# Issue order in a hybrid attention and Fourier encoder: one block of projection steps, the statistics of the next chunk, roundings, late weights and first loads are moved

## The chip, the cores and the metric

The kernel runs on one core of one Trainium2 chip. The metric is the device time of one execution in microseconds (us), the median of several runs. A difference of about 0.3% (4.9 us here) is what a measurement of this kernel can tell from no change.

TensorE is called PE below, its weight loads PEld; VectorE is DVE, ScalarE is ACT, GpSimd is POOL, and SyncE, which only issues transfers in this kernel, is SP. A "q" behind such a name is the engine's sequencer, which issues transfers and waits.

## The reference

```python
def attention_layer(x, g, w_in, w_out, sink, rel_bias):
    h = rmsnorm(x, g)
    z = h @ w_in                               # q, k, v and gate
...
    o = banded_gqa_with_sink(q, k, v, rel_bias, sink)
    return x + (o * jax.nn.silu(gate)) @ w_out

def fourier_layer(x, g, w_gate, w_out):
    h = rmsnorm(x, g)
    f = jnp.fft.fftn(hg, axes=(1, 3), norm="ortho").real   # over positions, and over each group of 256 channels
...
    return x + (f * jax.nn.silu(h @ w_gate)) @ w_out
```

Both layers run once, attention first, and a last rmsnorm follows. This is done for a prompt of 2048 positions and, apart from it, for a sample of 512 positions; the model width is 1024. Attention has 16 query heads of 64 channels, four to each key and value head, looks 128 positions back and ahead, adds a bias per distance and head, and counts one learned sink per head in the sum under the softmax. All values are float32.

## The kernel before, in words

Every float32 product is made as three products of rounded parts: a value is split into a high part (a cast by ACT) and a low part (a subtraction by DVE or POOL), and `matmul3` (lines 92 to 95) multiplies high by high, high by low and low by high. So most tiles come in two parts, and "rounding" below means the cast and the subtraction that follows it.

**Attention.** Positions are cut into five chunks of 512: the sample first (chunk 0), then four of the prompt. For a chunk, `make_h` (187) loads x transposed, one block of 128 channels (k) after the other, and splits it into h. `kv_proj` (287) makes keys and values. The 16 heads then go in eight pairs p; a pair is called a query here. `qg_proj` (369) gives each pair 16 steps on PE, eight for its query and eight for its gate, each step three matmuls over one k; after the eighth step of each half the result is taken out of PSUM (`evac_q`, `evac_g`). `attention` (410) has the parts of one pair's attention over 128-position blocks b: `scores`, `biased` (DVE adds the bias to the scores and finds the extreme value), `exps` (ACT), `divide`, `transp` (PE transposes), `parts` (ACT and DVE round the transposed weights), `av` (PE), `out_evac` (ACT copies half of the result, the tile `t`, DVE adds, POOL multiplies by the gate) and the `split` that `out_evac` returns (ACT rounds the gated result into `uT`, POOL or DVE makes its low part).

The loop over n (800 to 856) writes the order out by hand: 17 periods a chunk, each with two blocks of scores of the new half of a pair and the transposes and products of the half before. Projection steps are spread between them as filler: `ahead_n` steps run before the first period (16 in chunk 0, 12 in the others), the rest is shared out over 27 half periods by `quota`. At the end of each period four numbered extras run (`extra`, 784). Among them are the statistics of the next chunk (`stats`, 151): `one(i)` squares and sums tile i-1 of x on ACT (line 162) and loads tile i (166); when all are summed, `inv_rms` (86) makes the reciprocal roots, the first step on DVE (88), the second on POOL (89). In chunk 0 they start in period 6, in the later chunks in period 9; the fifth chunk has no next one. For chunk 0 itself they run at once, inside `kv_proj`.

**What sets the order.** Each engine runs its instructions in one fixed order. A planner makes that order from the order in the program, by costs that it assumes. `after(a, b)` (128) puts a behind b in the planner's eyes only; `seq(engine, ins)` (133) chains the instruction behind the last chained one of that engine. Scores, biased, exps, divide, parts, projection evacuations, the copy of `t` and the split's cast are all chained in this way. Squares, reciprocal roots, weight casts (114), x loads and weight loads are not: the planner puts them where it believes they fit. `keep_in_program_order` puts an instruction behind everything written before it on its engine.

**The start.** `half` (234) loads the first key weights in two halves, one on SP's and one on ACT's queue, ahead of the x tiles; each half is rounded by ACT (238) and DVE (239). `bias_rows` (247) loads three small tensors for the bias.

**Fourier phase and the turn.** `gates` (998) makes the gates with one level of Strassen's scheme. At the last call, `hooks` (1427 on) put other work between its products: the loads of the output weights (`f_load`, tiles `wo`), and the first Fourier harmonics over positions (`position`, 1195; `halves_of`, 1183, rounds its input `gl` into `gs`, lines 1190 and 1191). Output weights 0 to 7 come as stored parts; the rest is loaded as float32 (`w32f`, line 1412) and rounded by `f_split` (1414; ACT on 1418, DVE on 1419). After the gates come the harmonics 0 and 2 of the sample (`early`) and `finish` (1246), the output projection of two tiles.

Of the kernel before, what the change touches and what calls it, by code (L numbers as in the profile page):

```python
# [43 lines left out]
def encoder(  # L44
# [40 lines left out]

    def inv_rms(ss, n, name):
        inv = main.tile([P, 8], F32, tag="inv", bufs=2, name=name)
        DVE.tensor_scalar(inv[:, :n], ss[:, :n], 1.0 / D, EPS, ALU.mult, ALU.add)
        POOL.tensor_tensor(inv[:, :n], inv[:, :n], mhalf[:, :n], ALU.pow)
        return inv  # L90
# [37 lines left out]
    def after(ins, anchor):  # L128

        if anchor is not None:  # L130
            tc.add_manual_dep(ins.ins, anchor.ins.name, ISSUE, reason="issue order")
# [10 lines left out]
    def attention_phase():  # L142

        with ExitStack() as es:
# [6 lines left out]
            def stats(c):  # L151

                tok, lo_t, hi_t = CHUNKS[c]
                nt = min(640, hi_t - tok) // P
                ss = main.tile([P, 8], F32, tag="ss", bufs=2, name=f"ss{c}")

                xs = []

                def one(i):

                    if i:
                        sq = ACT.activation(xs[i - 1], xs[i - 1], AF.Square, accum_out=ss[:, i - 1 : i])
                        after(sq, last_exp[0])
                    if i < nt:
                        xs.append(xtile([P, D], F32, f"xs{c}_{i}"))
                        after(SP.dma_start(xs[i], x[tok + i * P : tok + (i + 1) * P, :]), last_exp[0])

                return [lambda i=i: one(i) for i in range(nt + 1)] + [lambda: inv_rms(ss, nt, f"inv{c}")]

# [16 lines left out]

            def make_h(c, invb, between={}):

# [3 lines left out]
                for k in range(KD):  # L192
# [4 lines left out]
                    else:  # L197
                        xk = xtile([P, D], F32, f"xk{c}_{k}")[:, :640]
                    SP.dma_start(xk[:, :n], xT[k * P : (k + 1) * P, tok : tok + n])
                    if invb is not None:  # L200
# [32 lines left out]

            def half(i):
                cs = slice(i * 512, i * 512 + 512)
                (SP, ACT)[i].dma_start(wk32[:, cs], w_in[8, :, cs])
                return lambda: (
                    tc.keep_in_program_order(ACT.copy(wk[:, 0, cs], wk32[:, cs])),
                    DVE.tensor_tensor(wk[:, 1, cs], wk32[:, cs], f32(wk[:, 0, cs]), ALU.subtract),
                )  # L240

            halves = [half(i) for i in range(2)]
            halves[0]()
            early = [(wk[:, 0], wk[:, 1])]
            hs, halo = make_h(0, None, {0: halves[1], 3: lambda: early.append(load_w(0, 9, "k0_1", DVE))})

            def bias_rows():

                rowd = dram.tile([NH, 512], F32, name="rowd")
                rb = ap.tile([33, NH], F32, tag="tmp", bufs=2, name="rb")  # L250
                DVE.memset(rb[32:33], 1.0)
                SP.dma_start(rb[:32], rel_bias)
                oh = ap.tile([33, 512], F32, tag="s", bufs=2, name="oh")
                SP.dma_start(oh, onehot)
                bp = bank("bp")
                PE.matmul(bp[:NH], rb, oh, start=True, stop=True)
                brow = ap.tile([NH, 512], F32, tag="tmp", bufs=2, name="brow")
                DVE.tensor_copy(brow, bp[:NH])

                POOL.dma_start(rowd, brow)  # L260
                sk = ap.tile([P, NH], F32, tag="sk", name="sk")
                SP.dma_start(sk, bass.AP(sink.tensor, sink.offset, [[0, P], [1, NH]]))
                DVE.tensor_scalar(sk, sk, -1.0, None, ALU.mult)
                return rowd, sk
# [480 lines left out]
            for c in range(len(CHUNKS)):  # L745
# [22 lines left out]

                ahead_n = 16 if c == 0 else 12
                chain.pop(PE, None)  # L770
# [29 lines left out]
                for n in range(17):  # L800
# [24 lines left out]
                    if new:  # L825
                        for j in range(2):
                            new[0].exps(new[1], j)
                        if n < 15:
                            for j in range(2):
                                new[0].biased(new[1] + 1, j)  # L830
                        new[0].divide(new[1], 0)
                        for j in range(2):
                            new[0].exps(new[1] + 1, j)
                        new[0].divide(new[1], 1)
                        for j in range(2):
                            new[0].divide(new[1] + 1, j)
                    for i in range(quota[2 * n] if n < 15 else 18 - n):
                        (work or op).pop(0)()
                    if split:
                        split()  # L840
                        split = None
                    if old:
# [18 lines left out]
    def fourier_phase(tail):  # L861
        with ExitStack() as es:
# [559 lines left out]
            def turn_first(i):  # L1422
# [9 lines left out]
                4: [lambda: f_load(4)],  # L1432
                5: [lambda: turn_first(0), lambda: f_load(5), lambda: f_split(4)],
                6: [lambda: turn_first(1), lambda: f_split(5)],
            })
            new = [t for p in early for t in position(*p)]
            for k in (6, 7):
# [223 lines left out]
```

## Time and profile before

| | |
|---|---|
| median of three runs | 1619.75 us (1616.98, 1619.75, 1622.47) |
| the profiled execution | 1622.4 us |
| its span, first to last instruction | 1620.6 us |
| mean granted TensorE clock | 0.995 of full speed |

The profile is of one execution. A row of a timeline gives the start in us from the span's start, the length in us, the engine, the line of the kernel, the operation, the tile written and the tiles read, the shapes and the count; in brackets stands how long the engine was idle before it and what ended that. In a shape such as 128x512 the first number is partitions.

### The profile page before, as it was taken

How to read it: one execution, taken by the hardware profiler on the slowest of the kernel's cores; microseconds unless marked ns; L12 is line 12 of the kernel's file. 1: busy time of each engine (PE TensorE's matmuls, PEld its weight loads, DVE VectorE, ACT ScalarE, POOL GpSimd, SP SyncE). 2: the span in 40 equal slices, each digit the busy share in tenths (PEclk: the TensorE clock that was granted, in tenths of full speed). 3: DMA queues.
4: the chain of work that ended last, by engine and by line, in shares of the span. 5: the costliest groups of instructions: out<-in, count | busy, mean ns of one | idle time of the engine just before them, and what ended most of it. 6: DMA issues, size and time to landing. Idle time of an engine off the chain costs nothing.

```text
span 1620.6 us, 27520 instructions
## 1 busy us (share of the span) xinstructions
PE 1598.9 (99%) x9835; PEld 1334.6 (82%) x9835; DVE 1116.6 (69%) x2799; ACT 870.2 (54%) x2043; POOL 431.1 (27%) x605
## 2 busy tenths in 40 slices
PE   9999999999999999999999999999999999999998
PEld 7777888888888888978788888888888887888886
DVE  6788665777547776367754577668576767988696
ACT  6687644676237674157752476546545554343252
POOL 2456551421403414024222242211112111100010
PEclk9999999999999999999999999999999999999999
DMA  7487696656765567655659566666456469455952
GB/s 300 157 314 272 227 351 218 227 215 211 287 220 197 214 237 259 225 205 214 242 166 326 203 219 228 236 217 248 170 208 241 172 220 407 153 195 195 348 201 91
DMA packets 100644, 374.16 MB, mean 231 GB/s; under 512 B 12139, under 2 KB 22379, under 8 KB 83100
## 3 DMA queue, kind: packets, MB, share of 16 engines
q1 hardware_dynamic: 81708, 297.91, 51.8%
q0 software_dynamic: 16464, 70.30, 11.1%
q10 hardware_dynamic: 2336, 4.20, 0.7%
q8 instruction: 78, 1.28, 0.3%
q14 instruction: 58, 0.48, 0.1%
HBM read 281.10 MB, written 91.26 MB: 230 GB/s over the span
## 4 chain that ended last, share of the span: by engine, by line
PE 87%; DMA 5%; DVE 4%; ACT 2%; issue 1%; POOL 1%; SPq 0%; POOLq 0%; DVEq 0%; ACTq 0%
PE qp L95 13%; PE gp L95 12%; PE op L95 8%; PE spt L95 8%; PE W L95 6%; PE spt L441 6%; PE av L525 6%; PE fo L95 5%; PE z L95 4%; PE vp L95 4%; PE Z L95 3%; PE pt L499 3%; PE Wo L95 2%; PE X L95 2%; PE trb L940 1%; DMA xs<-in_x_dram 1%
## 5 line engine op out<-in xcount | busy, mean ns | idle before, releaser
L95 PE MATMUL qp<-h,wq 128*128 128x512 f32 x960 | 239.9, 399 | 0.2 <-DVE pts L508 0.2
L95 PE MATMUL gp<-h,wg 128*128 128x512 f32 x960 | 237.7, 396 | 0.0
L460 DVE CUSTOM_DVE_ANT_0 S<-spt,b 128x385 f32<-128x385 f32 (+1 forms) x320 | 156.9, 527 | 115.6 <-PE spt L441 115.2
L507 ACT CAST pts<-pt 128x384 fp32r<-128x384 f32 (+1 forms) x320 | 123.8, 472 | 185.6 <-PE pt L499 185.4
L95 PEld LDWEIGHTS qp<-h,wq 128*128 128x128 f32 x960 | 176.6, 190 | 42.6 <-issue 5.2
L95 PEld LDWEIGHTS gp<-h,wg 128*128 128x128 f32 x960 | 175.2, 188 | 43.5 <-issue 9.7
L468 ACT ACTIVATE S<-S 128x385 f32<-128x385 f32 (+1 forms) x320 | 190.1, 605 | 35.6 <-DVE S L460 35.1
L508 DVE TENSOR_TENSOR pts<-pt,pts 128x384 fp32r<-128x384 f32 (+1 forms) x320 | 147.3, 522 | 25.7 <-ACT pts L507 24.7
L549 POOL TENSOR_TENSOR uT<-o,uT 128x256 fp32r<-128x256 f32 x75 | 55.5, 740 | 358.9 <-ACT uT L548 358.9
L95 PE MATMUL op<-wo,uT 128*128 128x512 f32 x600 | 140.4, 391 | 0.0
L95 PE MATMUL fo<-wo,tTu 128*128 128x512 f32 x576 | 140.3, 395 | 0.0
L441 PE MATMUL spt<-kwin,qab 64*128 64x384 f32 (+1 forms) x960 | 132.6, 358 | 5.7 <-DVE S L460 5.6
L95 PEld LDWEIGHTS op<-wo,uT 128*128 128x128 f32 x600 | 111.9, 188 | 23.9 <-issue 0.7
L95 PEld LDWEIGHTS fo<-wo,tTu 128*128 128x128 f32 x576 | 106.8, 190 | 20.5
L525 PEld LDWEIGHTS av<-pts,v 128*128 128x128 f32 x576 | 101.4, 188 | 19.0 <-DVE pts L508 0.4
L441 PEld LDWEIGHTS spt<-kwin,qab 64*128 64x128 f32 x960 | 85.1, 185 | 37.5 <-issue 27.5
L525 PE MATMUL av<-pts,v 128*128 128x512 f32 (+1 forms) x576 | 115.9, 341 | 0.0
L95 PE MATMUL spt<-wo,uT 128*128 128x512 f32 x360 | 86.7, 392 | 0.0
L480 DVE TENSOR_SCALAR S<-S 128x384 f32<-128x384 f32 (+1 forms) x192 | 79.2, 413 | 5.3
L543 DVE TENSOR_TENSOR o<-av,t 64x256 f32<-64x256 f32 x150 | 62.6, 417 | 26.4 <-ACT t L534 25.0
L95 PEld LDWEIGHTS spt<-wo,uT 128*128 128x128 f32 x360 | 66.5, 188 | 13.7
L499 PEld LDWEIGHTS pt<-ident,S 64*128 64x128 f32 x1792 | 68.8, 138 | 6.2 <-issue 2.3
(304 smaller groups left out, 2937.5 us busy)
## 6 DMA issues: line engine op xcount, KB each, us to landing
wo<-wsd SPq DMA_DIRECT2D x32, 1024.0 KB, 5.2
wq<-wsd SPq DMA_DIRECT2D x31, 1024.0 KB, 7.4
wg<-wsd SPq DMA_DIRECT2D x31, 1024.0 KB, 4.9
x<-x1d SPq DMA_DIRECT2D x40, 512.0 KB, 3.6
b<-b21d SPq DMA_DIRECT2D x40, 512.0 KB, 5.1
b<-rowd SPq DMA_DIRECT2D x40, 384.0 KB, 4.3
xs<-in_x_dram SPq DMA_DIRECT2D x23, 512.0 KB, 6.5
s2d<-gt POOLq DMA_DIRECT2D x40, 256.0 KB, 3.4
```

Of the source, the lines that this page charges most:

```text
L95: pe(PE.matmul(out, a[i], b[j], start=start and i + j == 0, stop=stop and i == 1, skip_group_check=more))
L441: pe(PE.matmul(banks[j][:, 2 + k0 * P : 2 + k1 * P], res["q"][rows, qp, b * P : (b + 1) * P], kwin[g][rows, kp, b * P + k0 * P : b * P + k ...
L460: seq(DVE, DVE.tensor_tensor_reduce(out=s[:, e0:e1], in0=ps[:, 1 + e0 : 1 + e1], in1=st["bias"][:, j, 386 - e1 : 386 - e0][:, ::-1], scale ...
L468: last_exp[0] = seq(ACT, ACT.activation(s[:, e0:e1], s[:, e0:e1], AF.Exp, bias=s[:, 386:387], scale=-1.0, accum_out=s[:, 387:388]))
L480: seq(DVE, DVE.tensor_scalar(s[:, ks], s[:, ks], den, None, ALU.mult))
L499: pe(PE.transpose(ps[h][:, kb, j, :], ss[j][rows, 1 + kb * P : 1 + (kb + 1) * P], ident[rows, rows]))
L507: seq(ACT, ACT.copy(hi, ps[:, k0:k1]))
L508: seq(DVE, DVE.tensor_tensor(lo, ps[:, k0:k1], f32(hi), ALU.subtract))
L525: pe(PE.matmul(to, v, pt, start=n == part == 0, stop=part == 1 and n in (1, len(todo) - 1), skip_group_check=n > 1,))
L543: seq(DVE, DVE.tensor_tensor(o[64 * j : 64 * j + 64], ps[0:64, :, j], t2[:, :, j], ALU.add))
L549: low = eng.tensor_tensor(lo, o, f32(hi), ALU.subtract)
L940: PE.transpose(ps[:, k * P : (k + 1) * P], self.x[i][:, c0 : c0 + P], ident)
```

## The change

Six things are moved, and no arithmetic changes.

1. Chunk 0 runs 20 projection steps before its first scores, not 16: four steps of the second pair's query.
2. The squares and the first step of the reciprocal roots, where they belong to chunks 1 to 4, are chained on ACT and DVE at the place where the program has them, the end of a period.
3. `split`, the rounding of the gated result, runs behind the first two exps of the period, not behind the filler before `av`.
4. At the turn, the rounding of output weights 4 and 5 stands behind the harmonics 0 and 2, not in the gates' hooks.
5. At the start, SP asks for the first x tile before anything else. The first half of the key weights comes in two quarters on ACT's queue, the second half on SP's queue behind the first x tile.
6. The loads of the three bias tensors and of chunk 0's x tiles for the statistics keep the program's order on SP.

```diff
@@ -83,9 +83,9 @@
     def htile(shape, dtype, name):
         return main.tile(shape, dtype, align_bytes=LINE, tag="hT", bufs=8, name=name)
 
-    def inv_rms(ss, n, name):
+    def inv_rms(ss, n, name, place=lambda ins: None):
         inv = main.tile([P, 8], F32, tag="inv", bufs=2, name=name)
-        DVE.tensor_scalar(inv[:, :n], ss[:, :n], 1.0 / D, EPS, ALU.mult, ALU.add)
+        place(DVE.tensor_scalar(inv[:, :n], ss[:, :n], 1.0 / D, EPS, ALU.mult, ALU.add))
         POOL.tensor_tensor(inv[:, :n], inv[:, :n], mhalf[:, :n], ALU.pow)
         return inv
 
@@ -160,12 +160,16 @@
 
                     if i:
                         sq = ACT.activation(xs[i - 1], xs[i - 1], AF.Square, accum_out=ss[:, i - 1 : i])
-                        after(sq, last_exp[0])
+                        if c:
+                            seq(ACT, sq)
                     if i < nt:
                         xs.append(xtile([P, D], F32, f"xs{c}_{i}"))
-                        after(SP.dma_start(xs[i], x[tok + i * P : tok + (i + 1) * P, :]), last_exp[0])
-
-                return [lambda i=i: one(i) for i in range(nt + 1)] + [lambda: inv_rms(ss, nt, f"inv{c}")]
+                        load = SP.dma_start(xs[i], x[tok + i * P : tok + (i + 1) * P, :])
+                        after(load, last_exp[0])
+                        if c == 0:
+                            tc.keep_in_program_order(load)
+
+                return [lambda i=i: one(i) for i in range(nt + 1)] + [lambda: inv_rms(ss, nt, f"inv{c}", lambda ins: seq(DVE, ins) if c else None)]
 
             def spread(c, inv, place=None):
 
@@ -184,7 +188,7 @@
                     ACT.copy(invb[:, i0 * P : (i0 + m) * P], ps[:, : m * P])
                 return invb
 
-            def make_h(c, invb, between={}):
+            def make_h(c, invb, between={}, first=None):
 
                 tok, lo_t, hi_t = CHUNKS[c]
                 n = min(640, hi_t - tok)
@@ -196,7 +200,9 @@
                         xk = xk2[:, k % 2]
                     else:
                         xk = xtile([P, D], F32, f"xk{c}_{k}")[:, :640]
-                    SP.dma_start(xk[:, :n], xT[k * P : (k + 1) * P, tok : tok + n])
+                    load = SP.dma_start(xk[:, :n], xT[k * P : (k + 1) * P, tok : tok + n])
+                    if first and k == 0:
+                        first(load)
                     if invb is not None:
                         last_mul[0] = POOL.tensor_tensor(xk[:, :n], xk[:, :n], invb[:, :n], ALU.mult)
                         after(last_mul[0], last_evac[0])
@@ -231,27 +237,29 @@
             wk = wp.tile([P, 2, D], F32R, align_bytes=LINE, tag="w", bufs=4, name="wk0_0")
             wk32 = stage[0]("w32k0_0")
 
-            def half(i):
-                cs = slice(i * 512, i * 512 + 512)
-                (SP, ACT)[i].dma_start(wk32[:, cs], w_in[8, :, cs])
+            def part(queue, c0, c1, behind=None):
+                cs = slice(c0, c1)
+                after(queue.dma_start(wk32[:, cs], w_in[8, :, cs]), behind)
                 return lambda: (
                     tc.keep_in_program_order(ACT.copy(wk[:, 0, cs], wk32[:, cs])),
                     DVE.tensor_tensor(wk[:, 1, cs], wk32[:, cs], f32(wk[:, 0, cs]), ALU.subtract),
                 )
 
-            halves = [half(i) for i in range(2)]
-            halves[0]()
+            quarters = [part(ACT, i * 256, i * 256 + 256) for i in range(2)]
             early = [(wk[:, 0], wk[:, 1])]
-            hs, halo = make_h(0, None, {0: halves[1], 3: lambda: early.append(load_w(0, 9, "k0_1", DVE))})
+            rest = []
+            hs, halo = make_h(0, None, {
+                0: quarters[1], 1: lambda: rest[0](), 3: lambda: early.append(load_w(0, 9, "k0_1", DVE)),
+            }, lambda x0: (rest.append(part(SP, 512, 1024, x0)), quarters[0]()))
 
             def bias_rows():
 
                 rowd = dram.tile([NH, 512], F32, name="rowd")
                 rb = ap.tile([33, NH], F32, tag="tmp", bufs=2, name="rb")
                 DVE.memset(rb[32:33], 1.0)
-                SP.dma_start(rb[:32], rel_bias)
+                tc.keep_in_program_order(SP.dma_start(rb[:32], rel_bias))
                 oh = ap.tile([33, 512], F32, tag="s", bufs=2, name="oh")
-                SP.dma_start(oh, onehot)
+                tc.keep_in_program_order(SP.dma_start(oh, onehot))
                 bp = bank("bp")
                 PE.matmul(bp[:NH], rb, oh, start=True, stop=True)
                 brow = ap.tile([NH, 512], F32, tag="tmp", bufs=2, name="brow")
@@ -259,7 +267,7 @@
 
                 POOL.dma_start(rowd, brow)
                 sk = ap.tile([P, NH], F32, tag="sk", name="sk")
-                SP.dma_start(sk, bass.AP(sink.tensor, sink.offset, [[0, P], [1, NH]]))
+                tc.keep_in_program_order(SP.dma_start(sk, bass.AP(sink.tensor, sink.offset, [[0, P], [1, NH]])))
                 DVE.tensor_scalar(sk, sk, -1.0, None, ALU.mult)
                 return rowd, sk
 
@@ -766,7 +774,7 @@
                 loads[0]()
                 at[0].start()
 
-                ahead_n = 16 if c == 0 else 12
+                ahead_n = 20 if c == 0 else 12
                 chain.pop(PE, None)
                 for s in work[:8]:
                     s()
@@ -825,6 +833,10 @@
                     if new:
                         for j in range(2):
                             new[0].exps(new[1], j)
+                    if split:
+                        split()
+                        split = None
+                    if new:
                         if n < 15:
                             for j in range(2):
                                 new[0].biased(new[1] + 1, j)
@@ -836,9 +848,6 @@
                             new[0].divide(new[1] + 1, j)
                     for i in range(quota[2 * n] if n < 15 else 18 - n):
                         (work or op).pop(0)()
-                    if split:
-                        split()
-                        split = None
                     if old:
                         old[0].av(old[1])
                         split = old[0].out_evac(old[1])
@@ -1430,10 +1439,13 @@
                 2: [lambda: f_load(2), lambda: early.append(sample(2, (1,), (left,), (xtile,), left))],
                 3: [lambda: first.extend(position(*one)), lambda: f_load(3)],
                 4: [lambda: f_load(4)],
-                5: [lambda: turn_first(0), lambda: f_load(5), lambda: f_split(4)],
-                6: [lambda: turn_first(1), lambda: f_split(5)],
+                5: [lambda: turn_first(0), lambda: f_load(5)],
+                6: [lambda: turn_first(1)],
             })
-            new = [t for p in early for t in position(*p)]
+            new = position(*early[0])
+            f_split(4)
+            new += position(*early[1])
+            f_split(5)
             for k in (6, 7):
                 f_load(k)
             for k in (6, 7):
```

## The prediction, made before the changed kernel was run

> **What bounds the kernel now.** The page's busy times say it first: TensorE.
>
> ```profile
> PE 1598.9 (99%) x9835; PEld 1334.6 (82%) x9835; DVE 1116.6 (69%) x2799; ACT 870.2 (54%) x2043; POOL 431.1 (27%) x605
> ```
>
> Of the span of 1620.6 us PE is idle for 21.7. No other engine comes near, and the change takes no matmul away, so it can win only idle time of PE, and slow time. The view of PE's waits from 5.6 to 1362.2 us says where the idle time is (who <- what ended the wait: us in total, times, longest).
>
> ```profile
> PE spt L441 <- DVE S L460: 5.6, 7, 2.0
> PE As L95 <- ACT gs L1190: 2.3, 1, 2.3
> PE pt L499 <- ACT xs L162: 1.2, 2, 0.8
> PE spt L95 <- ACT h L205: 1.2, 1, 1.2
> PE tru L894 <- DVE us L1228: 0.5, 1, 0.5
> PE pt L499 <- ACT pts L507: 0.4, 1, 0.4
> PE pt L499 <- DVE o L543: 0.4, 1, 0.4
> ```
>
> The large ones lie where the change works: scores (one wait of 2.0), the turn (2.3), squares (the waits on xs, pts and o), the start (1.2). Then I asked for the granted clock in stretches of 3.41 us around them (columns: stretch, length, PE busy and instructions, clock, DMA share, GB/s).
>
> ```profile
> 41.91:45.32 3.41, 1.39 (x13) 1.00 0.74 303
> 45.32:48.73 3.41, 3.41 (x12) 0.50 0.38 161
> 123.83:127.24 3.41, 2.10 (x30) 1.00 0.95 328
> 127.24:130.65 3.41, 3.41 (x9) 0.50 0.19 78
> 799.66:803.07 3.41, 2.38 (x35) 1.00 1.01 411
> 1359.45:1362.86 3.41, 1.15 (x7) 1.00 1.02 417
> 1362.87:1366.28 3.41, 3.41 (x11) 0.50 1.03 420
> ```
>
> Behind three idle places PE runs 3.41 us at half clock. From 127.24 it gets through about 8 matmuls of 512 columns in that time (9 touch the stretch); at full clock 12 take 2.91 us (the row of 58.23 below), so 8 take 1.9. Such a stretch costs 1.5 us beside the gap ahead of it, three cost 4.5. PE busy for 2.10 us of a stretch was too little; 2.38 was enough.
>
> The Trainium skill (TensorE: Matmul & The Clock Gate, section "HAM oscillation — how this bites in real kernels") draws the line at idle gaps of more than about 3.4 us. By that rule no gap here slows the clock, and the sum below would be 4.5 us smaller. The trace differs: gaps of 2.0 and 2.3 us, and one of 0.8 with one of 0.5, were enough.
>
> The three runs go from 1616.98 to 1622.47 us; the profiled execution took 1622.4 (its span and 1.8 around it). The range of 5.5 us is near the price of three slow stretches, so I take it that the faster runs had fewer of them. I count from the profiled execution, take its stretches off with their gaps, and hold the result against the median, 1619.75.
>
> **1. Four steps ahead of the first scores.** Three timelines, of PE, ACT and DVE:
>
> ```profile
> 42.16 0.79 PE L441 MATMUL spt<-kwin,qab 64*128 64x256 f32 x7
> 44.97 1.05 PE L441 MATMUL spt<-kwin,qab 64*128 64x384 f32 x5 [2.02 <-DVE S L460]
> ```
>
> ```profile
> 42.31 1.05 ACT L114 CAST wg<-w32g 128x1024 fp32r<-128x1024 f32 x1 [2.99 <-PE gp L95]
> ```
>
> ```profile
> 44.49 0.42 DVE L460 CUSTOM_DVE_ANT_0 S<-spt,b 128x257 f32<-128x257 f32 x1
> ```
>
> ```profile
> 58.23 2.91 PE L95 MATMUL gp<-h,wg 128*128 128x512 f32 x12
> ```
>
> The second scores need a bank that DVE frees by biased (L460). DVE comes to it only at 44.49, since the gate's evacuation ahead of it needs a tanh, which stands behind a weight cast on ACT. Four steps are 12 matmuls, 2.91 us: the first scores start at 45.07, when DVE is free. What is late next is one biased alone, as in the later chunks; the first scores of the second prompt chunk show 0.48:
>
> ```profile
> 475.83 0.79 PE L441 MATMUL spt<-kwin,qab 64*128 64x384 f32 x5 [0.48 <-DVE S L460]
> ```
>
> Gain 2.02 - 0.48 = 1.54 us, and a slow stretch. The steps are not additional: the filler of the 27 half periods falls from 104 steps to 100, so each later pair's weights are needed a little sooner. The four steps need the second pair's query weight; POOL ends its low part at 38.36 + 2.82 = 41.18, 1.0 us before the steps:
>
> ```profile
> 38.36 2.82 POOL L119 TENSOR_TENSOR wq<-w32q,wq 128x256 fp32r<-128x256 f32 x4
> ```
>
> If that cover goes, PE waits for what is missing. Bounds -3.5 to +1.0; I take -3.0.
>
> **2. Squares and norms at period ends.** In chunk 0 (ACT's timeline, then PE's waits from 123 to 127 us):
>
> ```profile
> 121.36 1.05 ACT L162 ACTIVATE xs<-xs 128x1024 f32<-128x1024 f32 x1
> ```
>
> ```profile
> PE pt L499 <- ACT xs L162: 0.8, 1, 0.8
> PE spt L441 <- DVE S L460: 0.5, 1, 0.5
> ```
>
> That square stands ahead of the copy of `t` on ACT. The copy frees a bank for PE's transposes, so the square's 1.05 us shows as 0.8 on PE. Behind the copy it delays parts at most. The 0.5 is a norm that stands ahead of biased on DVE. In chunk 3:
>
> ```profile
> 801.40 1.06 ACT L162 ACTIVATE xs<-xs 128x1024 f32<-128x1024 f32 x1 [1.81 <-DMA xs<-in_x_dram]
> ```
>
> ```profile
> 802.59 0.17 DVE L88 TENSOR_SCALAR inv<-ss 128x4 f32<-128x4 f32 x1 [2.04 <-ACT xs L162]
> ```
>
> ```profile
> 803.33 0.79 PE L441 MATMUL spt<-kwin,qab 64*128 64x384 f32 x5 [1.29 <-DVE S L460]
> ```
>
> The norm holds DVE's line for 2.04 us, since its square waits for x; biased stands behind it, and PE loses 1.29. Chained, the norm comes at the end of the next period. Chunks 1 and 2 lose 0.4 each to a square ahead of `t`. So: 1.3 and a stretch of 1.5 in chunk 0, 2.1 in chunks 1 to 3.
>
> What the chain adds: where a square waits for x, all of ACT's chain waits behind it, parts and exps first, and DVE's low parts, and PE's av. ACT's room at a period's end, in chunk 1, is one square (1.06) and the idle time here:
>
> ```profile
> 360.29 1.03 ACT L507 CAST pts<-pt 128x256 fp32r<-128x256 f32 x3 [0.71 <-PE pt L499]
> ```
>
> That is 1.8 us, where two squares want 2.1; PE's filler between transposes and av (12 matmuls, 2.91 us) covers the rest, as it covers the 1.81 of chunk 3 now. In chunk 0 a weight cast that waits for its transfer stays ahead of parts, and the slow clock hid it: up to 1.5 may come back. Bounds for part 2: -5.3 to +1.5; I take -4.5.
>
> **3. Roundings behind the first exps.** From ACT's waits, and from the view of line 548 (its duration min/median/max; below, who waited for it):
>
> ```profile
> ACT S L468 <- DVE S L460: 35.1, 71, 3.4
> ```
>
> ```profile
> L548 ACT CAST uT<-o x75: 387/392/441, 67.3 to 1049.7; 128x256 fp32r<-128x256 f32 x75
> ...
>   POOL uT L549: 358.9, 65
> ```
>
> Between the two pairs of exps ACT is idle for DVE, 35.1 / 71 = 0.49 us a time, and the cast of 0.39 fits in. It needs POOL's product of the period before; POOL now sits idle behind that product for 358.9 / 65 = 5.5 us, so it is done in time in most periods. PE has no idle time to win by it. If POOL is late, the second exps wait. Bounds -0.5 to +1; I take 0.
>
> **4. Weights behind the harmonics.** ACT, then PE:
>
> ```profile
> 1360.27 1.14 ACT L1418 CAST wo<-w32f 128x512 fp32r<-128x512 f32 x2 [2.40 <-DMA w32f<-in_w_fout_dram]
> 1361.31 0.61 ACT L1190 CAST gs<-gl 128x512 fp32r<-128x512 f32 x1
> ```
>
> ```profile
> 1361.98 0.39 PE L95 MATMUL As<-gs,tbs 128*128 128x260 f32 x1 [2.26 <-ACT gs L1190]
> ```
>
> ACT waits 2.40 us for a weight, and the rounding that PE needs stands behind it. With the order turned round, PE goes on with harmonics and a half projection that need none of these weights. Late next are the last weights themselves, which still come at the pace of the transfers (share 1.02 above). Gain 2.26 and a stretch of 1.5; bounds -3.8 to +1; I take -3.7.
>
> **5. First x first.** PE, then PEld:
>
> ```profile
> 6.66 6.57 PE L95 MATMUL spt<-h,wk 128*128 128x512 f32 x26 [1.16 <-ACT h L205]
> ```
>
> ```profile
> 12.73 0.30 PEld L95 LDWEIGHTS spt<-h,wk 128*128 128x128 f32 x2 [0.18 <-DVE h L206]
> ```
>
> The same bytes cross the same two queues before PE can start, and the first weights, now on ACT's queue, still come behind the transfer issued there first. An earlier start would run into the fifth k, for which the weight loads wait already, at 12.73. Bounds: 0.3 earlier, or 0.4 later and a slow stretch with it (+1.9); I take 0. **6.** The pinned loads had that order: 0.
>
> Sum: 3.0 + 4.5 + 3.7 = 11.2; 1622.4 - 11.2 = 1611.2, rounded 1611. That is 8.7 us or 0.54% under the median.
>
> **The rivals.** *Half of it*: the gaps of chunk 0 and of the turn come back elsewhere, since transfers set them. Then 1.54 and 2.1 of gaps and one stretch go: 1622.4 - 5.1 = 1617.3, no change against the median. For it: DMA shares of 0.95 to 1.03 at both places; against it: PE has other work there. *The plan shifts*: the planner puts everything unchained by its own costs, so gaps that are small now grow by as much as the removed ones shrink, and the change doesn't do what it says: 1619, no change. *A late start*: 1611 + 1.9 = 1613. *Slower*: chained squares stop ACT. How long such an x tile takes from issue to landing (view of the tile xs), and that SP issues two well ahead:
>
> ```profile
> DMA to landing us min/median/max: 4.9/6.5/10.6
> ```
>
> ```profile
> 349.62 2.28 SPq L166 DMA_DIRECT2D xs<-in_x_dram  x2
> ```
>
> If a load is issued only 3 us before its square's place and takes 10.6, ACT stands for 7.6; take 1.8 of room and 2.9 of filler off, and PE loses 2.9 and a stretch of 1.5. Once in each of four chunks that is 17.6 us: 1628. It decides where x lands more than 4.7 us after the copy of `t`. Against it: the loads of 349.62 are some 9 us ahead of the end of their period.
>
> **How the numbers follow.** Forecast 0.58; late start 0.08; half of it 0.12; shifted plan 0.10; slower 0.12. The first two are faster by over 0.3% (about what a measurement can tell from no change; under 1614.9): 0.66. The next two lie within it: 0.22. Slower: 0.12. The range: the lower bounds of parts 1 to 5 give 1622.4 - 13.4 = 1609.0, and a median may lie 2 us off, so 1607; above it takes in the late start, half of it and the shifted plan, 1619. Only the slower case and the edges are left out.
>
> **What would show it.** Right: PE's waits hold no 2.0 and no 2.3, biased ends waits of about 0.5, no half-clock stretch after the start, a span near 1609. Part 1 is wrong if first scores still wait over 0.6 in chunk 0; part 2 if ACT's waits on x grow and PE waits for parts or in av; part 3 if ACT waits for POOL at L548; part 4 if PE waits for a `wo` rounding after 1360; part 5 if the first real matmul starts after 6.7. The whole is wrong if PE's idle time is as large as before at other places.

## The result, and the profile after

The forecast was 1611 us; the changed kernel takes 1627.35 us, the median of four runs (1624.80, 1626.63, 1628.06, 1628.07), where the kernel before took 1618.99 beside it. The ratio is 1.0043, with a 95% interval of 1.0031 to 1.0056: slower by 0.43%. The profiled execution took 1624.8 us, the least of the four.

The busy times of the changed kernel, then its view of PE's waits in the same window as before (5.6 to 1362.2 us; us in total, times, longest; the lines of the code stand up to 9 further down).

```profile
PE 1597.4 (98%) x9835; PEld 1331.8 (82%) x9835; DVE 1141.0 (70%) x2800; ACT 871.8 (54%) x2044; POOL 438.0 (27%) x605
```

```profile
PE spt L449 <- DVE S L468: 3.8, 6, 1.6
PE pt L507 <- DVE s L406: 2.2, 2, 1.7
PE qp L95 <- DVE pts L516: 1.7, 1, 1.7
PE pt L507 <- DVE o L551: 1.7, 3, 1.2
PE spt L449 <- DVE qab L397: 1.7, 1, 1.7
PE spt L95 <- ACT h L211: 1.1, 1, 1.1
...
PE pt L507 <- DVE qab L397: 0.5, 1, 0.5
PE gp L95 <- DVE pts L516: 0.4, 1, 0.4
```

The waits of 2.0 and 2.3 us that the change aimed at are gone, and five new ones of 1.2 to 1.7 us stand there. All the new ones lie in chunk 0, and all end on DVE. The one on L516 stands at 121 us behind a square that waited 2.46 us for x; the others come with slow copies on DVE, at least in part, as one period shows below. The first scores of chunk 0 wait 0.35 us:

```profile
46.31 0.79 PE L449 MATMUL spt<-kwin,qab 64*128 64x384 f32 x5 [0.35 <-DVE S L468]
```

DVE has the same work as before but for one instruction, and is busy for 24 us more (1116.6 before).

Where the time went is best seen by stages. The table gives each profiled execution in us: from the first matmul on h to chunk 1's first scores (chunk 0), from there to chunk 4's first scores (chunks 1 to 3), from there to the end, and how many 3.41-us stretches at half clock lie before the tail. The runs e1 to e16 are told below.

| | chunk 0 | chunks 1 to 3 | rest | stretches |
|---|---|---|---|---|
| before | 255.25 | 640.43 | 718.29 | 3 |
| after | 261.01 | 637.51 | 717.49 | 1 |
| after, again (e5) | 265.04 | 637.77 | 717.34 | 4 |
| before + four steps (e11) | 264.58 | 640.29 | 717.15 | 4 |
| before + squares (e15) | 253.44 | 639.24 | 715.93 | 0 |
| before + roundings (e14) | 258.50 | 639.63 | 714.46 | 2 |
| before + turn (e10) | 253.48 | 640.38 | 716.49 | 0 |
| best version (e13) | 254.54 | 637.65 | 715.90 | 2 |

In its two profiled executions the change gains 2.9 and 2.7 us in chunks 1 to 3 and loses 6 and 10 in chunk 0. The stretches at half clock differ from execution to execution, so PE's waits say more: from 40 to 200 us they add up to 3.9 us before, 10.2 after and 9.9 in e11. One period of chunk 0 shows how. Four timelines of the changed kernel: DVE, POOL, ACT, PE.

```profile
74.25 2.64 DVE L430 COPY b<-sk 128x2 f32<-128x2 f32 x1
76.78 0.16 DVE L431 COPY b<-sk 128x2 f32<-128x2 f32 x1
```

```profile
72.88 2.83 POOL L119 TENSOR_TENSOR wq<-w32q,wq 128x256 fp32r<-128x256 f32 x4
75.68 0.73 POOL L119 TENSOR_TENSOR wg<-w32g,wg 128x256 fp32r<-128x256 f32 x1
76.36 0.57 POOL L123 DMA_DIRECT2D wsd<-wq  x1
```

```profile
77.57 0.62 ACT L486 ACTIVATE S<-S 128x384 f32<-128x384 f32 x1 [2.24 <-DVE S L484]
78.21 0.58 ACT L542 COPY t<-av 64x512 f32<-64x512 f32 x1
```

```profile
79.89 0.25 PE L507 MATMUL pt<-ident,S 64*128 64x64 f32 x1 [1.18 <-DVE o L551]
81.83 0.40 PE L507 MATMUL pt<-ident,S 64*128 64x64 f32 x6 [1.69 <-DVE s L406]
```

A copy of two values per partition, the sink's edge of the bias tile, takes 2.64 us on DVE; its twin right behind it takes 0.16. The long one begins while POOL makes low parts of weights, and ends when POOL turns to issuing a transfer. DVE's divides stand behind it, ACT waits 2.24 us for them, the copy of `t` comes late, and PE's transposes wait 1.18 us for the bank that DVE's additions free. Then the evacuation of a gate, which now falls at the end of the period, holds the next bank for 1.69.

The same copy in the kernel before, and POOL beside it:

```profile
75.09 1.44 DVE L422 COPY b<-sk 128x2 f32<-128x2 f32 x1
```

```profile
73.68 2.82 POOL L119 TENSOR_TENSOR wq<-w32q,wq 128x256 fp32r<-128x256 f32 x4
76.80 0.57 POOL L123 DMA_DIRECT2D wsd<-wq  x1 [0.30 <-POOL wq L119]
```

Here POOL runs dry behind the query's low parts, the copy takes 1.2 us less, and PE does not wait at all. What differs ahead of it on ACT is the place of the gate's cast. It stood in the middle of the period:

```profile
73.31 1.07 ACT L114 CAST wg<-w32g 128x1024 fp32r<-128x1024 f32 x1
```

In the changed kernel it stands ahead of the parts, and POOL goes straight on with the first of the gate's low parts before it issues the transfer:

```profile
70.49 1.05 ACT L114 CAST wg<-w32g 128x1024 fp32r<-128x1024 f32 x1
```

POOL did not wait for that cast in the kernel before: it ended at 74.38, and POOL was free only at 76.50. It is the order on POOL that differs. The two go together in ten traces (late cast and early transfer in before, e1, e14 and e15, the other way round in after, e3, e5, e6, e8 and e11); that the planner makes POOL's order from the place of the cast is argued, not shown.

### The profile page after: what moved, and what is told of

It reads as the page before. It is cut to its first block, busy times and chain, and to the rows that moved or that the text cites. A ratio compares the mean times of both kernels' runs of the same rounds, so it can differ in the third digit from the quotient of the medians.

```text
span 1623.0 us, 27525 instructions
## 1 busy us (share of the span) xinstructions
PE 1597.4 (98%) x9835; PEld 1331.8 (82%) x9835; DVE 1141.0 (70%) x2800; ACT 871.8 (54%) x2044; POOL 438.0 (27%) x605
## 4 chain that ended last, share of the span: by engine, by line
PE 82%; DVE 5%; issue 5%; DMA 4%; ACT 2%; POOL 1%; SPq 0%; POOLq 0%; DVEq 0%; ACTq 0%
PE qp L95 13%; PE gp L95 13%; PE op L95 8%; PE spt L95 8%; PE spt L449 6%; PE av L533 6%; PE W L95 4%; PE fo L95 4%; PE vp L95 4%; PE pt L507 3%; PE z L95 3%; PE Wo L95 2%; PE Z L95 2%; DMA xs<-in_x_dram 1%; PE X L95 1%
## 5 line engine op out<-in xcount | busy, mean ns | idle before, releaser
L516 DVE TENSOR_TENSOR pts<-pt,pts 128x384 fp32r<-128x384 f32 (+1 forms) x320 | 147.4, 523 | 27.5 <-ACT pts L515 26.8
L553 POOL TENSOR_TENSOR o<-o,s 128x256 f32<-128x256 f32 x75 | 55.2, 736 | 153.1 <-DVE o L551 152.8
L488 DVE TENSOR_SCALAR S<-S 128x384 f32<-128x384 f32 (+1 forms) x192 | 89.4, 465 | 5.3
```

What stands on the lines that cost most here:

```text
L488: seq(DVE, DVE.tensor_scalar(s[:, ks], s[:, ks], den, None, ALU.mult))
L516: seq(DVE, DVE.tensor_tensor(lo, ps[:, k0:k1], f32(hi), ALU.subtract))
L553: eng.tensor_tensor(o, o, s, ALU.mult)
```

## The experiments

Three theories of the loss in chunk 0. **Lock**: DVE's plain copies in SBUF stand still as long as POOL works, and the change brings them beside longer trains of POOL. **Places**: four more steps move every evacuation of a projection by half a query, to the ends of the periods. **Squares**: chained squares wait for x, the rival "slower" of the prediction. Runs of one group share a chip and the runs of the kernel before, with medians of 1620.93 (e1 to e4), 1619.98 (e5 to e8), 1621.03 (e9 to e12) and 1621.57 us (e13 to e16).

**e5: the changed kernel again.**

> The changed kernel itself, on the chip of this group, as the measure for the three others. All theories: 6 to 8 us above the kernel before.

Measured: 1626.55 us, ratio 1.0038 (1.0023 to 1.0052). The loss is there in another group of runs, too.

**e1: 16 steps.**

```diff
-                ahead_n = 20 if c == 0 else 12
+                ahead_n = 16 if c == 0 else 12
```

> The changed kernel with 16 steps ahead of chunk 0's first scores instead of 20. Three theories of what chunk 0 lost. Places: the four steps move every projection evacuation of chunk 0 by half a query, to the ends of the periods, and with them the weight casts and POOL's trains of low parts; then most of the loss goes: the first scores wait 2.0 us again, but the waits of 0.5 to 1.7 us at 61, 79, 80, 91, 99, 100 and 138 us go, and the time falls by 5 to 8 us, to about 1620. Copies: DVE's copies of the sink into the bias tile (line 430) stand behind POOL's low parts whatever the steps; then the waits at 79 to 80, 99 to 100 and 138 stay and the time rises by 1.7, to about 1629. Squares: those of chunk 1, chained, wait for x; then only the wait on first scores changes, 1629 as well.

Measured: 1621.51 us, ratio 1.0002 (0.9987 to 1.0017). Without the four steps the loss is gone, although the copies still meet POOL (one took 2.82 us at 131.81, and PE waited 2.04 behind it).

**e2: the copies on ACT.**

```diff
-                    DVE.tensor_copy(bt[:, :, 0], sk[:, 2 * p : 2 * p + 2])
-                    DVE.tensor_copy(bt[:, :, 385], sk[:, 2 * p : 2 * p + 2])
+                    ACT.copy(bt[:, :, 0], sk[:, 2 * p : 2 * p + 2])
+                    ACT.copy(bt[:, :, 385], sk[:, 2 * p : 2 * p + 2])
```

> The changed kernel with the two copies of the sink into the bias tile (lines 430 and 431) on ACT instead of DVE. Copies: in the changed kernel three of them took 2.6, 2.3 and 2.5 us while POOL made low parts of weights (0.16 where POOL was idle), and PE then waited 1.18 + 1.69, 0.30 + 1.65 and 1.68 us, one half-clock stretch of 1.5 behind the last; on ACT they wait for nobody, so these 8.0 us go and the time is about 1619 to 1620. Places: the evacuations at the ends of periods cost the same without the copies; the waits stay within 2 us in sum, 1626 to 1628. Squares: no change beyond 1 us.

Measured: 1620.96 us, ratio 0.9996 (0.9986 to 1.0006). With all 20 steps in place, moving 80 tiny copies gives the whole loss back.

**e6: the copies in another form, on DVE.** The instruction keeps its engine, and only its form changes.

```diff
-                    DVE.tensor_copy(bt[:, :, 0], sk[:, 2 * p : 2 * p + 2])
-                    DVE.tensor_copy(bt[:, :, 385], sk[:, 2 * p : 2 * p + 2])
+                    none = ap.tile([P, 2], F32, tag="none", bufs=1, name=f"none{c}_{p}")
+                    for e, col in enumerate((0, 385)):
+                        DVE.tensor_scalar(
+                            bt[:, :, col], sk[:, 2 * p : 2 * p + 2], 1.0, None, ALU.mult, ALU.add, accum_out=none[:, e : e + 1],
+                        )
```

> The changed kernel with the two copies of the sink still on DVE and in their places, but in the form that chunk 0's divides have: a multiplication (by 1.0) that also sums into an accumulator. Lock: a plain copy in SBUF can't run beside POOL's instructions, and in chunk 0's divides the accumulating form never took more than 0.62 us beside POOL; then the copies take 0.15 to 0.3 us, PE's waits at 79 to 80, 99 to 100 and 138 us shrink as with the copies on ACT, and the time is 6 us below the changed kernel. Place: DVE stands there for another reason (what the copy reads, or a buffer that it waits for); then the copies keep 2.3 to 2.8 us and the time stays that of the changed kernel.

Measured: 1620.46 us, ratio 1.0000 (0.9991 to 1.0010). The views of the two lines, first of the changed kernel, then of e6 (duration in ns, min/median/max; first and last start):

```profile
L430 DVE COPY b<-sk x40: 149/426/2643, 15.8 to 1008.2; 128x2 f32<-128x2 f32 x40
```

```profile
L432 DVE TENSOR_SCALAR_CACHE_REDUCE b<-sk x80: 133/153/198, 15.7 to 1004.4; 128x2 f32<-128x2 f32 x80
```

127 of the 160 instructions of that line (copy and read of the accumulator) ran beside POOL in e6, and none took over 0.20 us. It is the form of the copy that waits, not its place or its data. The lock is shown. From 40 to 200 us PE's waits add up to 6.6 us in e6: 0.35 at the first scores, 1.6 behind evacuations, 1.2 behind biased, and 3.5 behind squares that waited for x. The kernel before has 3.9, so the change does not win there even without the lock.

The Trainium skill (SBUF — State Buffer, section "Who interferes with whom") says why: DVE and GpSimd share a pair of SBUF ports, held exclusively for a whole instruction; copies and `tensor_scalar` can take that pair, but not the form that also writes out its accumulator. The durations above agree: up to 2.64 us for the plain form, at most 0.20 for the other. The page has the loser wait until the other's instruction is done; here the copy waited through up to five instructions of POOL in a row (e14 below). The measurement decides.

**e7: copies on ACT and 16 steps.** The edits of e1 and e2 together.

> The changed kernel with the copies of the sink on ACT and with 16 steps ahead. Each of the two alone brought the time back by some 6 us. One loss: the steps only brought the copies beside the trains, so both together bring no more than one, 6 to 7 us below the changed kernel, with the wait of 2.0 us on the first scores. Two losses: both together bring 10 to 12, some 5 us below the kernel before.

Measured: 1619.06 us, ratio 0.9993 (0.9981 to 1.0004). The two causes are one loss for the most part: undoing both brings 7.5 us against e5, not 10 to 12.

**e8: 24 steps.** `ahead_n = 24`.

> The changed kernel with 24 steps ahead of chunk 0's first scores: the second pair's whole query, so the evacuations stand half a query away from those with 20, as they did with 16, and the first scores wait 0.35 us. Places: the waits at the ends of periods (0.47 at 61, 0.45 at 91) go, and as far as the trains follow the evacuations also those at 79, 80, 99 and 100; the time is 6 to 8 us below the changed kernel, or 1.7 to 3 below that with 16 steps. More steps ahead are only worse, since the later weights are needed sooner: trains and copies meet as with 20, and the time is within 2 us of the changed kernel.

Measured: 1630.54 us, ratio 1.0063 (1.0046 to 1.0081). The evacuations stand in the old rhythm again, and the time is the longest of all, 4.0 us above e5: neither outcome of the expectation. The waits at 61 and 91 us go, those about 80 and 100 stay, and copies took up to 3.41 us. The first scores wait 1.76 us, since the second query's evacuation now stands there, and the longest wait of all stands behind a chained square that waits for x (ACT, then PE):

```profile
126.70 1.06 ACT L162 ACTIVATE xs<-xs 128x1024 f32<-128x1024 f32 x1 [2.65 <-DMA xs<-in_x_dram]
```

```profile
129.66 1.32 PE L449 MATMUL spt<-kwin,qab 64*128 64x384 f32 x5 [4.83 <-DVE S L468]
```

So this run alone does not settle the theory of places; e2 and e6 do, where the evacuations stand as with 20 steps and the loss is gone. The theory had a part of truth: in e6, without the lock, PE still waits 0.46, 0.67 and 0.45 us behind evacuations, and 20 steps are no better than 16 (e9 against e12, and e6 against e7, whose copies run on ACT).

**e3: the split back.** The split stands behind the filler again.

> The changed kernel with the rounding of the gated result (split) back behind the filler, ahead of av, as before. If the earlier cast sends POOL's low part of it beside DVE's copies and divides in SBUF, which lost DVE 24 us in all, then DVE's busy time falls from 1141 to about 1117 us, and if the same meeting makes the three long copies of chunk 0, the time falls by up to 8, to 1620. If the long copies come from the weights' trains and not from the split, DVE's busy time falls by about 15 us but PE's waits of chunk 0 stay: 1626 to 1628.

Measured: 1627.26 us, ratio 1.0039 (1.0027 to 1.0051). DVE's busy time falls to 1121.1 us, and the loss stays. So 20 of the 24 us come from the earlier split, which puts 67 of the 80 copies beside POOL (10 with the split back); the copies themselves take 9 of the 20 (30.0 against 20.7 us in all), and the plain `tensor_scalar` of the later chunks' divides 10 (89.4 against 79.3). In the later chunks, where such a copy takes 0.70 us at most, they cost PE nothing.

**e4: chunk 1's squares free.**

```diff
-                        if c:
+                        if c > 1:
                             seq(ACT, sq)
+                        else:
+                            after(sq, last_exp[0])
```

The norm's chain was taken off for chunk 1 too.

> The changed kernel with the squares and the norm of chunk 1 (which run in chunk 0) free of the chain, as before; those of chunks 2 to 4 stay chained. Squares: PE's waits of 0.45 at 111.9 and 1.72 us at 121.3, behind squares that waited 1.55 and 2.46 us for x, go, 2.2 us, and up to 1.5 with a half-clock stretch in some executions: 1624 to 1625. Copies or places: the waits at 79 to 100 and 138 us stay. If the squares were the whole loss, about 1619.

Measured: 1625.10 us, ratio 1.0030 (1.0018 to 1.0041), which the intervals do not tell from the changed kernel. The free squares waited 1.67 and 3.23 us for x, and PE waited 0.6 and 2.2 behind them. So x is as late here whether or not the squares are chained. ACT's waits on x from 40 to 200 us, of before, after, before with chained squares (e15), before with the four steps (e11), and after with the split back (e3):

```profile
ACT xs L162 <- DMA xs<-in_x_dram: 1.3, 1, 1.3
```

```profile
ACT xs L162 <- DMA xs<-in_x_dram: 4.0, 2, 2.5
```

```profile
ACT xs L162 <- DMA xs<-in_x_dram: 1.0, 1, 1.0
```

```profile
ACT xs L162 <- DMA xs<-in_x_dram: 0.9, 1, 0.9
```

```profile
ACT xs L162 <- DMA xs<-in_x_dram: 0.7, 1, 0.7
```

Neither the four steps alone nor the chain alone makes x late; it is late where the four steps and the earlier split come together (4.0 to 7.2 us in after, e5, e4, e6 and e2; 2.7 with the 24 steps of e8). And e11 and e3 lose as much as the changed kernel without that wait, so the squares are not the loss.

**e9 and e12: later squares.** Accumulating copies, and chunk 1's statistics from period 9 on (`i >= 38` for all chunks); e12 with 16 steps.

> The changed kernel with the accumulating copies and with the statistics of chunk 1 begun in period 9 of chunk 0, as in the later chunks, instead of period 6. With the accumulating copies alone ACT still stood 2.5 and 3.6 us for x ahead of chained squares, and PE 1.4 and 2.1 us behind them. Squares: if x lands late because the weights of the later pairs cross the queues in periods 6 to 8, these 3.5 us go, and up to 1.5 of a half-clock stretch: about 1616 to 1617, 3 to 4 under the kernel before. If x is as late in periods 9 to 11, the waits move there and the time stays at 1620 to 1621.

Measured: 1621.04 us, ratio 0.9995 (0.9982 to 1.0007). The gain did not come: x still came 1.60 us late for one square, and new waits of 1.47 and 0.94 us appeared at 158 to 160 us.

> As the run with late squares and accumulating copies, but with 16 steps ahead. With the lock gone the four steps should be worth what the forecast took, 1.5 us and a half-clock stretch in some executions: 1.5 to 3 us more than with 20 steps. If the evacuations at period ends (0.47, 0.67 and 0.45 us with 20 steps, absent with 16) cost as much, the two are equal within 1 us.

Measured: 1619.25 us, ratio 0.9987 (0.9974 to 1.0000), neither of the two outcomes: against e9, the four steps cost 1.8 us where the forecast had a gain.

**The parts alone, put into the kernel before.**

e11, part 1.

> The kernel before with 20 steps ahead of chunk 0's first scores and nothing else changed. Forecast: 3.0 us less. Lock: the later weights' rounding moves ahead with the steps, the copies of the sink meet longer trains of POOL (2.3 to 2.8 us in place of 1.3 to 1.7), and PE waits 5 to 6.5 us in chunk 0 that it did not wait before, against 1.7 to 3 won at the first scores: 2 to 5 us more. If the loss needs the other parts too (the earlier split, the chained squares), the time falls by 2 to 3.

Measured: 1629.15 us, ratio 1.0046 (1.0031 to 1.0062). The largest waits of PE from 40 to 200 us:

```profile
PE spt L441 <- DVE S L460: 2.5, 3, 1.7
PE pt L499 <- DVE o L543: 2.4, 2, 1.5
PE pt L499 <- DVE s L398: 2.2, 2, 1.7
```

These are waits of the changed kernel, and the copy ahead of the one at 80 us is slow here, too:

```profile
74.16 2.52 DVE L422 COPY b<-sk 128x2 f32<-128x2 f32 x1
```

One constant makes a loss as large as that of the whole change (7.5 us, more than the 2 to 5 expected); no other part is needed.

e15, part 2.

> The kernel before with part 2 alone: squares and norms of chunks 1 to 4 chained at period ends. Forecast: 4.5 us less, 1615.5 where the kernel before has 1620. Traces: 1.3 less in chunks 1 to 3; in chunk 0 the squares find the x tiles as late as the free ones do, so no gain there, or 1 to 2 us of new waits behind the chain: 1.3 less to 1 more. The rival by which chained squares stop ACT would have 8 more.

Measured: 1616.71 us, ratio 0.9972 (0.9959 to 0.9984). The forecast of 4.5 us was met; the traces had given 1.3 less to 1 more. PE's waits from 355 to 905 us fall from 3.5 us in three rows to 2.0:

```profile
PE spt L442 <- DVE S L461: 1.5, 3, 0.5
PE av L526 <- DVE pts L509: 0.3, 1, 0.3
PE av L526 <- ACT pts L508: 0.2, 1, 0.2
```

From 40 to 200 us they do not fall: 3.9 before, 4.3 here.

e14, part 3.

> The kernel before with part 3 alone: the split behind the first exps. Forecast: nothing. By the traces (chunks 1 to 3 took 639.1 us with squares chained and the split in its old place, 637.4 to 637.8 with both) 1.4 us less in chunks 1 to 3. Lock: DVE's copies move beside POOL in most periods and take 0.4 us in place of 0.16, which costs nothing unless a train of weights stands there, in chunk 0, where it can cost 1 to 3. So 1.4 less to 2 more.

Measured: 1623.26 us, ratio 1.0015 (1.0004 to 1.0026). The earlier cast sends POOL's low part of the split into the train of the weights. DVE and POOL:

```profile
132.93 3.85 DVE L422 COPY b<-sk 128x2 f32<-128x2 f32 x1
```

```profile
132.77 2.83 POOL L119 TENSOR_TENSOR wg<-w32g,wg 128x256 fp32r<-128x256 f32 x4
135.57 0.72 POOL L549 TENSOR_TENSOR uT<-o,uT 128x256 fp32r<-128x256 f32 x1
136.24 0.57 POOL L123 DMA_DIRECT2D wsd<-wg  x1
```

The copy stands for five instructions, until POOL issues a transfer, and PE waits 2.33 us behind it.

e10, part 4.

> The kernel before with part 4 alone, the rounding of output weights 4 and 5 behind the harmonics. Forecast: the wait of 2.26 us and its half-clock stretch go, 3.7 us less, 1616 where the kernel before has 1620. The trace of the changed kernel lost 0.56 + 0.17 there for others, so 2.5 to 3.1 is more likely. If the transfers of the weights set the end of this stage, nothing is gained: 1620.

Measured: 1619.99 us, ratio 0.9998 (0.9987 to 1.0009). No gain that can be measured. PE's waits at the turn (1340 to 1400 us) in e10, then in e15 and e14, where the turn is as it was before:

```profile
PE As L95 <- ACT us L1224: 0.7, 1, 0.7
...
PE Bs L95 <- DVE us L1226: 0.2, 1, 0.2
```

```profile
PE As L95 <- ACT gs L1191: 1.8, 2, 1.7
```

```profile
PE As L95 <- ACT gs L1191: 0.5, 1, 0.5
```

The wait that was to go was 2.26 us in one execution, 1.7 and 0.5 in others, and what takes its place is 0.8.

e16, the accumulating copies in the kernel before.

> The kernel before with the accumulating copies alone. In its trace three copies of chunk 0 took 1.3, 1.4 and 1.7 us beside POOL's trains, and PE waited nowhere behind them, except in some executions about 1 us at 133. So no change: within 1 us. If the lock costs there as well, 2 to 3 less.

Measured: 1620.28 us, ratio 0.9993 (0.9984 to 1.0003). There the copies cost nothing that can be measured, as the trace said.

**e13: the version that the runs point to.** The changed kernel with 16 steps, accumulating copies, and chunk 1's squares and norm free.

> The changed kernel with 16 steps ahead, the accumulating copies, and the squares and the norm of chunk 1 free of the chain: chunk 0 as before, the later chunks as changed. If the gains of the later chunks add up (2.9 us in the traces of chunks 1 to 3, nothing at the turn), about 1617, 2.5 to 3 under the kernel before. If the free squares move chunk 0's waits elsewhere, as free and chained squares did alike with 20 steps, 1619 to 1620.

Measured: 1616.46 us, ratio 0.9970 (0.9960 to 0.9981). It beats both kernels, by about 5 and 11 us; but part 2 alone (e15) does as well within the intervals.

## Why the prediction was wrong

The four parts that were run alone give +0.46, -0.28, +0.15 and -0.02%, in sum +0.31%, against +0.43% (0.31 to 0.56) for the whole. The forecast had -0.54% against the median.

1. **The step that failed is part 1.** Forecast: -3.0 us, bounds -3.5 to +1.0; alone it is +7.5 (0.0046 of 1620; 5.0 to 10.0). The nearby effect came as worked out: the first scores wait 0.35 us, not 2.02. But "each later pair's weights are needed a little sooner" was named and priced at nothing. I checked that the one weight was ready for the four steps, and not whom the earlier rounding of all the others would meet. DVE's copies were in no part of the argument, although the trace of before held three of them at 1.3 to 1.7 us where 0.16 is normal. That was the row to follow. With the four steps alone (e11) such copies stand up to 2.52 us beside POOL, and PE's waits from 40 to 200 us grow from 3.9 to 9.9 us.
2. **Part 2** came out at its number: -4.5 forecast, -4.5 alone (-2.6 to -6.6). The traces show only a part of the way. Chunks 1 to 3 brought 1.2 us of the 2.1. In chunk 0 other waits took the place of those that went; e15's trace has no half-clock stretch there where that of before has two, and one of these two follows the wait on the first scores, which part 2 leaves at 2.02 us. Where the rest of the 4.5 comes from is open, and part of the agreement may be luck. Its loss beside part 1 was named as a rival. There x came late for chained and free squares alike, and it cost PE 2.2 us in the profile after, not 17.6. That this rival's 1628 lies next to the measured 1627.35 is luck: the loss has another cause.
3. **Part 3** was to be 0 (-0.5 to +1). Alone it costs 2.4 us (0.6 to 4.2), by the same lock: POOL's work was moved, and I counted only what POOL itself waits for. In the traces it gains in chunks 1 to 3 (640.4 before, 639.6 alone) and loses in chunk 0 (258.5).
4. **Part 4** was to bring 3.7; alone it brings 0.3 (a loss of 1.5 to a gain of 2.1). The mechanism worked, the size was off. The gap and its stretch were read from one execution, and others have less of both.
5. **Part 5** came out at nothing: the first matmul on h starts at 7.02 us in the profile after, 0.36 later than before, but between 6.5 and 7.25 in the other executions, with the old start as with the new. **Part 6** was not tried alone.

The sum had a second fault. It started from an execution with three half-clock stretches and took all three off. That execution is 3.5 us above the median of its runs (1622.47 against 1618.99), and e10 and e15 show executions of nearly the same code with none. Of the three, only what a typical execution has could be gained.

Not tried: what makes x late where the four steps and the earlier split come together. Two x tiles take 13 to 14 us there from issue to landing, and 9.5 was measured for one of them before; but with 16 steps (e1) they took 10 and 14, and ACT waited 1.6. That earlier weight transfers fill the queues is argued only.

## What to carry to other kernels

A constant that sets how far one engine runs ahead also moves every load, cast and rounding that feeds it: follow these into the engines where they land, not only to the engine that they serve. An instruction that takes ten times its normal duration is worth following even where nothing waits for it yet: here it was a shared resource showing itself. Price stalls over several executions where a single one can hold up to four slow-clock stretches.

## What the runs showed of the hardware

A plain copy on DVE can stand through several instructions of POOL: 0.16 us alone, 2.64 and 3.85 us beside four and five instructions in a row, ending when POOL turned to issuing a transfer. The same values moved by an accumulating form took at most 0.20. It does not always wait for such a pause. In the later chunks a copy ended with the one instruction of POOL that it met, although POOL went straight on (DVE, then POOL, profile after):

```profile
953.94 0.70 DVE L430 COPY b<-sk 128x2 f32<-128x2 f32 x1
```

```profile
953.88 0.74 POOL L557 TENSOR_TENSOR uT<-o,uT 128x256 fp32r<-128x256 f32 x1 [2.31 <-ACT uT L556]
954.58 1.55 POOL L635 TENSOR_TENSOR w32e<-w32e,w32e 128x256 f32<-128x256 f32 x2
```

What decides between the two was not found.

Whether an idle gap of PE costs a half-clock stretch depends on where it falls. The three stretches of the profile before begin at 45.32, 127.24 and 1362.87 us, 24 and 362 times 3.413 us apart: they lie on a grid. In every other trace with more than one stretch the starts lie a whole number of such steps apart, too. The same gap of 2.02 us ahead of the first scores stands in e16 and in e1. In e16 it falls into one step of the grid (columns: stretch, length, busy time and instructions of PE, PEld, DVE, ACT and POOL, clock, DMA share, GB/s):

```profile
42.29:45.70 3.41, 1.39 (x13) 0.94 (x12) 2.08 (x6) 2.22 (x5) 2.18 (x4) 1.00 0.75 308
45.70:49.11 3.41, 3.41 (x9) 2.67 (x9) 3.06 (x14) 2.12 (x7) 1.16 (x2) 0.50 0.46 195
```

In e1, whose grid is laid back from its one stretch at 136.55, it is split over two steps, and the clock stays:

```profile
40.98:44.39 3.41, 2.38 (x15) 1.56 (x13) 1.48 (x4) 1.54 (x2) 2.92 (x5) 1.00 0.69 276
44.39:47.80 3.41, 2.43 (x12) 1.89 (x13) 3.00 (x14) 2.26 (x8) 2.82 (x5) 1.00 0.65 271
```

PE was busy for 1.39 us of a step in the one, for 2.38 and 2.43 in the other. Between lies no sharp line in PE's busy time: 2.19 us in the step from 113.54 in e14 was followed by half clock, 1.70 in that from 121.27 in the changed kernel was not. The grid lies elsewhere in each execution, and with it the 1.5 us: that this is the spread of the runs, 1624.8 to 1628.1 for the changed kernel, fits and was not shown.
